# Normalising x by rows and turning it on TensorE, in the front of a hybrid attention layer

## The chip, the core and the metric

The kernel runs on one core of one Trainium2 chip. Time is device time in microseconds (us) of one execution; the kernel before took 860.34 us, the median of three runs (858.98 to 860.87). The engines are called PE (TensorE, with PEld for its weight loads), DVE (VectorE), ACT (ScalarE), POOL (GpSimd) and SP (SyncE, which here only issues transfers).

## What is computed

One layer over x (512 tokens, 1024 channels) and mem (256 memory tokens): three attention branches (gated linear attention "GLA", forgetting attention "FoX", cross attention into mem), merged by gates, an output projection, a squared-ReLU MLP and a last norm. The parts that the change touches:

```python
def rmsnorm(x, g):
    r = lax.rsqrt(jnp.mean(xf * xf, axis=-1, keepdims=True) + EPS)
    return (xf * r) * g

u = rmsnorm(h, g_mix[l])                    # h = x here
proj = u @ w_in[l]                          # feeds all three branches
...
mkv = rmsnorm(mem, g_mem[l]) @ w_mem_kv[l]
mk, mv = jnp.split(mkv, 2, axis=-1)         # memory keys, memory values
```

## The kernel before, in words

All matrix products run in a split of float32 into a high and a low part (`hi`, `lo`, type fp32r), three matmuls for each product (`mm3`, L122 to L124). A weight chunk of 128x1024 floats (512 KB) is loaded by SP (`load_w`, L108), its `hi` is cast on ACT (L114) and its `lo` is subtracted on DVE (L115); the pools hold three chunks of `raw`, of `hi` and of `lo`, so a cast into the fourth waits until PE has done with the first. `gT` makes one feature tile by tokens (one step for each of 8 contraction tiles); `gN` makes tokens by 512 features, chunk after chunk, with one PSUM bank for each token tile.

PE's order is the order of the code. The other engines' instructions are ordered by a scheduler when the program is built; `tc.issue_after(...)` keeps a group of them behind a given instruction.

The front (the pool `front`, L238 to L340) goes like this:

- mem and x come feature-major (features on partitions, `memr` and `xr`). SP loads mem in four parts between the parts of key chunk 0, then key chunks 1 and 2, half of x, chunk 3, the other half of x, chunk 4 (the first of the values), constants, and the later chunks.
- mem's values times the gain are split into `mxh` and `mxl` without the norm's factor, which is put in afterwards.
- `mk_proj` (L308) makes memory keys of one head; between the four of them, ACT squares mem and x and POOL and DVE add the squares up (`sq_cols`, L177). `rms_cols` (L189) sums over the partitions by matmuls with a column of ones (L195), and `rsqrt` (L198) makes a mean on DVE and a power of -0.5 on POOL. `bcast_rows` (L205) brings these factors to all partitions as a row: a diagonal matrix on ACT (L210), a matmul with ones (L211), a copy (L212).
- The memory values (`mv`, L325) are 48 matmuls over four chunks, with x's sum and x's row of factors between them.
- Then, for each of 8 feature tiles, u = x times gain times row is made on DVE or POOL (L335, L337) and split into `uhi` (ACT) and `ulo` (DVE).
- `g_proj` (L361) is the first product that wants u: 16 matmuls (L369, L370) for the low-rank decay and forget columns.

Behind the front, `fox_pair(0)` (L425) makes queries and keys of the first two FoX heads, 48 matmuls; `mem_split` (L342) puts mem's factors into the memory keys and splits keys and values. `decay_logs` (L380) makes log-sigmoids from the gate columns: four small matmuls (L383), absolute values, exponentials, and logarithms on ACT, the last with a load of another function table. `v_chunks` (the values of FoX, called `fv`) needs four PSUM banks of the pool `pmm`, which has four; the last one that comes free is that of the FoX keys, when `k_evac` (L438) has copied the second half out of it.

Of the kernel before, what the change touches and what calls it, by code (L numbers as in the profile page):

```python
# [58 lines left out]


@with_exitstack
def hybrid_block(ctx, tc, chunks, wst, xT, memT, xN, cols, gffn, gfin, wup, cst, out):
    nc = tc.nc
    PSUM = bass.MemoryType.PSUM
    index = {c: i for i, c in enumerate(chunks)}
# [3 lines left out]
    def nm(s):  # L69
        uid[0] += 1  # L70
        return f"{s}_{uid[0]}"
# [13 lines left out]
    def at_(shape=None):  # L85
        return pa.tile(shape or [P, 512], F32, tag="a", name=nm("a"))
# [67 lines left out]
    def run(*gens):  # L154
        for g in gens:
            for _ in g:
                pass
# [16 lines left out]
        nc.scalar.copy(hi, src)  # L174
        return nc.vector.tensor_tensor(lo, src, f(hi), op=ALU.subtract).ins  # L175

    def sq_cols(pool_, src, n, k, accs, pool_ks, tag):  # L177

        e = 1 if k in pool_ks else 0
        eng = nc.gpsimd if e else nc.vector  # L180
        if accs[e] is None:
            accs[e] = pool_.tile([P, n], F32, tag=f"{tag}_acc{e}", name=nm("acc"))
            nc.scalar.activation(accs[e], src[:, k, :], AF.Square)
        else:
            sq = pool_.tile([P, n], F32, tag=f"{tag}_sq{e}", name=nm("sq"), bufs=2)
            nc.scalar.activation(sq, src[:, k, :], AF.Square)
            eng.tensor_tensor(accs[e], accs[e], sq, op=ALU.add)

    def rms_cols(pool_, accs, n):  # L189

        accs = [a for a in accs if a is not None]
        ps = at_()
        for t in range(n // P):
            for i, a in enumerate(accs):
                nc.tensor.matmul(ps[:, t:t + 1], a[:, t * P:(t + 1) * P], ones[:, 0:1], start=i == 0, stop=i == len(accs) - 1)  # L195
        return rsqrt(pool_, ps[:, :n // P], 1.0 / D, n // P)

    def rsqrt(pool_, ss, inv, n):  # L198
        ms = pool_.tile([P, n], F32, tag="ms", name=nm("ms"), bufs=2)
        r = pool_.tile([P, n], F32, tag="rr", name=nm("rr"), bufs=2)  # L200
        nc.vector.tensor_scalar(ms, ss, inv, EPS, op0=ALU.mult, op1=ALU.add)
        nc.gpsimd.tensor_tensor(r, ms, mhalf[:, :n], op=ALU.pow)
        return r
# [33 lines left out]

    with pool("front") as fp:  # L238
        rmb = gv[:, 0, 0:M]
        rxb = fp.tile([P, S], F32, name="rxb")  # L240
        memr = fp.tile([P, KT, M], F32, name="memr")
        xr = fp.tile([P, KT, S], F32, name="xr")
        pre = {}

        def lead(key, n, i):
            if key not in pre:
                late = index[key] > 2
                pre[key] = [(fp if late else wp).tile([P, 1024], F32, tag="lead" if late else "raw", name=nm("raw"),
                                                      bufs=2 if late else 3)]
                pre[key] += [wp.tile([P, 1024], F32R, tag=g, name=nm(g)) for g in ("hi", "lo")]  # L250
            sl = slice(i * 1024 // n, (i + 1) * 1024 // n)
            raw, hi, lo = (t[:, sl] for t in pre[key])
            nc.sync.dma_start(raw, wst[index[key]][:, sl])
            nc.scalar.copy(hi, raw)
            nc.vector.tensor_tensor(lo, raw, f(hi), op=ALU.subtract)
# [12 lines left out]
        macc, xacc = [None, None], [None, None]  # L268
# [18 lines left out]
        nc.sync.dma_start(wup_s, wup)  # L287
        nc.sync.dma_start(cmask, cst[:, 6 * P + 8:])
        for k in range(KT):
            sq_cols(fp, memr, M, k, macc, range(KT), "m")  # L290
# [7 lines left out]
        UP = (2, 5)  # L298
# [6 lines left out]
        def mk_raw(h):  # L305
            return gkT[h // 2][:, (h % 2) * M:(h % 2) * M + M]

        def mk_proj(h):  # L308
            run(gT(("T", "w_mem_kv", P * h), mxh, mxl, lambda ps: nc.scalar.copy(mk_raw(h), ps[:, :M]), n=M))
            for k in (2 * h, 2 * h + 1):  # L310
                sq_cols(fp, xr, S, k, xacc, (1, 2, 3), "x")
                if k in UP:
                    nc.scalar.mul(xr[:, k, :], xr[:, k, :], gmix[:, k:k + 1])

        def mv_evac(t, ps):
            nc.scalar.mul(gqT[t], ps, rm[:, t:t + 1])

        mk_proj(0)
        mk_proj(1)
        rm = rms_cols(fp, macc, M)  # L320
        mk_proj(2)
        bcast_rows(fp, rm, M, rmb)
        mk_proj(3)
        nc.vector.tensor_copy(msk_s.rearrange("p a b -> p (a b)"), cst_s[:, 4 * P:6 * P])
        mv = gN([("N", "w_mem_kv", 2 * j, 512) for j in range(4)], of(mxh, mxl), 2, mmt, mv_evac)  # L325
        for _ in range(2):
            next(mv)
        rx = rms_cols(fp, xacc, S)
        for _ in range(5):
            next(mv)  # L330
        bcast_rows(fp, rx, S, rxb)
        for k in range(KT):
            ut = fp.tile([P, S], F32, tag="ut", name=nm("ut"), bufs=3)
            if k in UP:
                nc.gpsimd.tensor_tensor(ut, xr[:, k, :], rxb, op=ALU.mult)  # L335
            else:
                nc.vector.scalar_tensor_tensor(ut, xr[:, k, :], gmix[:, k:k + 1], rxb, op0=ALU.mult, op1=ALU.mult)  # L337
            u_end = split(uhi[:, k, :], ulo[:, k, :], ut)
        run(mv)
        get_w = get_plain  # L340

        def mem_split():  # L342
            for h in range(4):
                mk_evac(h)
            for t in range(2):
                split(mvh[:, t, :], mvl[:, t, :], gqT[t])

# [4 lines left out]
    with pool("fox") as xp:  # L352
# [668 lines left out]
def layout(inputs):  # L1021
# [26 lines left out]
    def tl(a):  # L1048
# [22 lines left out]
    cst[:, 6 * P:6 * P + 8] = -0.5  # L1071
    cst[:, 6 * P + 8:] = np.where(t > s, np.float32(NEG), 0.0)
    arrays = {
        "wst": wst, "xT": tl(x), "memT": tl(mem), "xN": np.ascontiguousarray(x), "cols": cols,
        "gffn": np.ascontiguousarray(np.broadcast_to(np.asarray(inputs["g_ffn"])[0], (P, D))),
        "gfin": np.ascontiguousarray(np.broadcast_to(np.asarray(inputs["g_final"]), (P, D))),
        "wup": wup, "cst": cst,
# [24 lines left out]
```

## Time and profile before

| what | value |
|---|---|
| time before, median of three runs | 860.34 us (858.98 to 860.87) |
| the profiled execution's own time | 859.26 us |
| its span in the trace | 857.1 us |
| PE busy / DVE busy / ACT busy / POOL busy | 840.5 / 498.4 / 404.3 / 87.4 us |
| mean granted PE clock | 0.995 |
| moved by DMA | 108.28 MB |

The span is what the trace shows from the first to the last instruction; the other 2.16 us lie around it. Matmuls are pipelined and their ends are modelled, so the distance of two starts tells more than a length. A bracket behind an instruction gives the idle time of its engine just before, and what ended it. The granted clock is TensorE's, as a share of full speed. Times in the timeline count from the start of the span.

### The profile page before, as it was taken

What the parts mean: (1) busy time and instruction counts of PE and PEld (TensorE: products, weight loads), DVE (VectorE), ACT (ScalarE), POOL (GpSimd) and SP (SyncE); (2) the same over time, 40 slices, a digit from 0 to 9 for tenths busy, and PEclk for the clock granted to TensorE, in tenths of its full rate; (3) what the DMA queues carried; (4) which work ended last, traced back from release to release, by engine and by line L of the source; (5) the groups of instructions that cost most, each with busy time, mean ns of one, the idle gap of its engine ahead of it and who ended that gap; (6) DMA issues with size and microseconds to landing.
All of it is one profiled execution on the core that took longest, in us unless ns stands there. A gap on an engine that the chain in (4) does not pass through costs nothing.

```text
span 857.1 us, 10630 instructions
## 1 busy us (share of the span) xinstructions
PE 840.5 (98%) x4041; PEld 695.4 (81%) x4041; DVE 498.4 (58%) x832; ACT 404.3 (47%) x646; POOL 87.4 (10%) x96
## 2 busy tenths in 40 slices
PE   8899999999999999999999999999999999999995
PEld 5778788888888888787888889888888888888884
DVE  5775657766444556574533546665556645665577
ACT  8764747754332431322332434655455345535642
POOL 5100000000000011211112100011001000110022
PEclk9999999999999999999999999999999999999998
DMA  8433232322222122124222413969435933791156
GB/s 319 151 123 125 106 115 99 123 75 75 76 96 99 53 96 75 50 74 172 99 98 99 172 50 124 318 122 238 155 97 122 273 123 83 149 281 53 26 102 168
DMA packets 32146, 108.28 MB, mean 126 GB/s; under 512 B 3872, under 2 KB 4832, under 8 KB 32096
## 3 DMA queue, kind: packets, MB, share of 16 engines
q1 hardware_dynamic: 24832, 84.00, 27.3%
q0 software_dynamic: 5472, 18.35, 12.2%
q10 hardware_dynamic: 1792, 5.26, 1.8%
q8 instruction: 32, 0.52, 0.2%
q14 instruction: 18, 0.15, 0.1%
HBM read 103.90 MB, written 2.13 MB: 124 GB/s over the span
## 4 chain that ended last, share of the span: by engine, by line
PE 90%; ACT 3%; DVE 3%; DMA 1%; issue 1%; POOL 0%; SPq 0%; DVEq 0%; POOLq 0%; ACTq 0%
PE mm L122 25%; PE mm L123 24%; PE mm L124 24%; PE a L123 3%; PE a L124 3%; PE a L122 3%; PE a L739 1%; DMA h<-G 1%; PE a L756 1%; PE a L499 1%; PE a L498 1%; PE a L750 1%; DMA memr<-in_memT_dram 1%; PE a L467 1%; PE a L466 1%
## 5 line engine op out<-in xcount | busy, mean ns | idle before, releaser
L115 DVE TENSOR_TENSOR wlo<-raw,whi 128x1024 fp32r<-128x1024 f32 x103 | 129.9, 1264 | 133.4 <-ACT whi L114 131.7
L114 ACT CAST whi<-raw 128x1024 fp32r<-128x1024 f32 x103 | 108.4, 1053 | 168.6 <-PE mm L123 128.4
L122 PE MATMUL mm<-uhi,whi 128*128 128x512 f32 x352 | 139.7, 397 | 0.0
L124 PE MATMUL mm<-uhi,wlo 128*128 128x512 f32 x352 | 137.6, 391 | 0.0
L123 PE MATMUL mm<-ulo,whi 128*128 128x512 f32 x352 | 137.5, 391 | 0.0
L122 PE MATMUL mm<-u2h,whi 128*128 128x512 f32 x240 | 93.4, 389 | 0.0
L123 PE MATMUL mm<-u2l,whi 128*128 128x512 f32 x240 | 93.4, 389 | 0.0
L124 PE MATMUL mm<-u2h,wlo 128*128 128x512 f32 x240 | 93.4, 389 | 0.0
L175 DVE TENSOR_TENSOR lo<-raw,hi 128x1024 fp32r<-128x1024 f32 x42 | 51.2, 1224 | 49.6 <-ACT hi L174 49.1
L124 PEld LDWEIGHTS mm<-uhi,wlo 128*128 128x128 f32 x352 | 66.2, 188 | 14.2
L122 PEld LDWEIGHTS mm<-uhi,whi 128*128 128x128 f32 x352 | 66.4, 189 | 13.5 <-issue 0.7
L123 PEld LDWEIGHTS mm<-ulo,whi 128*128 128x128 f32 x352 | 66.3, 188 | 12.9
L174 ACT CAST hi<-raw 128x1024 fp32r<-128x1024 f32 x42 | 44.0, 1053 | 62.5 <-PE mm L123 23.5
L979 POOL DMA_DIRECT2D raw<-in_wst_dram x32 | 28.1, 877 | 277.2 <-DVE lo L175 208.0
L123 PEld LDWEIGHTS mm<-u2l,whi 128*128 128x128 f32 x240 | 45.0, 188 | 9.4
L122 PEld LDWEIGHTS mm<-u2h,whi 128*128 128x128 f32 x240 | 45.0, 188 | 9.3
L124 PEld LDWEIGHTS mm<-u2h,wlo 128*128 128x128 f32 x240 | 45.0, 188 | 9.3
L122 PE MATMUL mm<-hi,ch 128*128 128x512 f32 x120 | 46.7, 389 | 0.0
L123 PE MATMUL mm<-lo,ch 128*128 128x512 f32 x120 | 46.7, 389 | 0.0
L124 PE MATMUL mm<-hi,cl 128*128 128x512 f32 x120 | 46.7, 389 | 0.0
L590 POOL TENSOR_TENSOR acc<-acc,th 128x512 f32<-128x512 f32 x16 | 24.0, 1503 | 102.7 <-DVE th L589 102.7
L668 POOL MEMSET qpos<- 64x512 f32 x2 | 1.0, 524 | 268.6 <-PE mm L124 268.6
(320 smaller groups left out, 1641.1 us busy)
## 6 DMA issues: line engine op xcount, KB each, us to landing
raw<-in_wst_dram SPq DMA_DIRECT2D x144, 512.0 KB
raw<-in_wst_dram POOLq DMA_DIRECT2D x32, 512.0 KB, 5.3
nFb<-dF ACTq DMA_DIRECT2D x8, 512.0 KB
xr<-in_xT_dram SPq DMA_DIRECT2D x4, 512.0 KB
h<-in_xN_dram SPq DMA_DIRECT2D x4, 512.0 KB
memr<-in_memT_dram SPq DMA_DIRECT2D x4, 256.0 KB
h<-G POOLq DMA_DIRECT2D x4, 256.0 KB, 5.7
out_dram<-h ACTq DMA_DIRECT2D x4, 256.0 KB
```

Of the source, the lines that this page charges most:

```text
L114: nc.scalar.copy(hi, raw)
L115: nc.vector.tensor_tensor(lo, raw, f(hi), op=ALU.subtract)
L122: nc.tensor.matmul(ps, lh, rh, start=start, stop=False)
L123: nc.tensor.matmul(ps, lh, rl, start=False, stop=False)
L124: nc.tensor.matmul(ps, ll, rh, start=False, stop=stop)
L174: nc.scalar.copy(hi, src)
L175: return nc.vector.tensor_tensor(lo, src, f(hi), op=ALU.subtract).ins
L466: nc.tensor.matmul(ps[:, :w], q, K[e][:, 0, :w], start=True, stop=False)
L467: nc.tensor.matmul(ps[:, :w], q, K[e][:, 1, :w], start=False, stop=True)
L498: nc.tensor.matmul(po[:, q0:], vv, PTh[:, c0:c0 + w], start=n == 0, stop=False)
L590: nc.gpsimd.tensor_tensor(acc[j], acc[j], th, op=ALU.add)
L979: nc.gpsimd.dma_start(raw[to, i], wst[index["B", q, i, x]], accum_op=ALU.add)
```

## The change

- x is no longer loaded feature-major; it comes as it is (`xn`, tokens on partitions, four tiles of 128 tokens, 512 KB each, from `xN`), behind key chunk 3 instead of around it.
- Between the four key projections, `x_norm(t)` squares a token tile on ACT with the sum along the row, makes the factor (`rsqrt`, mean on DVE and power on POOL), and scales the tile in place on DVE.
- `u_turn(k)` turns one feature tile: four PE transposes into one PSUM bank, then ACT writes `uhi` (times gain) and DVE writes `ulo`, both from PSUM. Two of them stand ahead of each chunk of the memory values.
- The four key projections stay in their PSUM banks until ACT copies them out behind the last `uhi`. The values use two banks of the pool `pa` instead of `pmm`, and are copied out without the factor.
- mem's statistics move: two squares on ACT (1024 wide) behind the last `uhi`, three additions on DVE; sum and factor (`mem_rms`) on PE behind `g_proj`; the row of factors (`mem_rows`) behind the first step of `fox_pair(0)`; `mem_split` behind that pair.

```diff
-        for j in range(4):
-            nc.sync.dma_start(xr[:, 2 * j:2 * j + 2], xT[:, 2 * j:2 * j + 2])
-            if j == 1:
-                lead(chunks[3], 1, 0)
+        lead(chunks[3], 1, 0)
+        for t in range(NT):
+            nc.sync.dma_start(xn[:, t, :], xN[t * P:(t + 1) * P, :])
         lead(chunks[4], 1, 0)
...
+        def x_norm(t):
+            sq = fp.tile([P, D], F32, tag="xsq", name=nm("xsq"), bufs=2)
+            nc.scalar.activation(sq, xn[:, t, :], AF.Square, accum_out=ssx[:, t:t + 1])
+            r = rsqrt(fp, ssx[:, t:t + 1], 1.0 / D, 1)
+            nc.vector.tensor_scalar(xn[:, t, :], xn[:, t, :], r, None, op0=ALU.mult)
+
+        def u_turn(k):
+            pt = at_()
+            for t in range(NT):
+                nc.tensor.transpose(pt[:, t * P:(t + 1) * P], xn[:, t, k * P:(k + 1) * P], ident)
+            a = nc.scalar.mul(uhi[:, k, :], pt, gmix[:, k:k + 1]).ins
+            return a, nc.vector.scalar_tensor_tensor(ulo[:, k, :], pt, gmix[:, k:k + 1], f(uhi[:, k, :]), op0=ALU.mult,
+                                                  op1=ALU.subtract).ins
+
+        for h in range(4):
+            mk_proj(h)
+            x_norm(h)
+        mv = gN([("N", "w_mem_kv", 2 * j, 512) for j in range(4)], of(mxh, mxl), 2, at_, lambda t, ps: nc.scalar.copy(gqT[t], ps))
+        for k in range(KT):
+            u_act, u_end = u_turn(k)
+            if k % 2:
+                run(islice(mv, 4))
+        with tc.issue_after(u_act):
+            for h in range(4):
+                nc.scalar.copy(mk_raw(h), kps[h][:, :M])
+        run(mv)
...
+        macc, rm, dg = gv[:, 2, :M], gv[:, 1, :2], gv[:, 3, :M]
+        msq = [fp.tile([P, 4, M], F32, name=f"msq{h}") for h in range(2)]
+        with tc.issue_after(u_act):
+            for h in range(2):
+                nc.scalar.activation(msq[h], memr[:, 4 * h:4 * h + 4, :], AF.Square)
+        nc.vector.tensor_tensor(msq[0], msq[0], msq[1], op=ALU.add)
+        nc.vector.tensor_tensor(msq[0][:, :2, :], msq[0][:, :2, :], msq[0][:, 2:, :], op=ALU.add)
+        nc.vector.tensor_tensor(macc, msq[0][:, 0, :], msq[0][:, 1, :], op=ALU.add)
+
+        def mem_rms():
+            ps = at_()
+            for t in range(2):
+                nc.tensor.matmul(ps[:, t:t + 1], macc[:, t * P:(t + 1) * P], ones[:, 0:1], start=True, stop=True)
+            nc.vector.tensor_scalar(rm, ps[:, :2], 1.0 / D, EPS, op0=ALU.mult, op1=ALU.add)
+            nc.gpsimd.tensor_tensor(rm, rm, mhalf[:, :2], op=ALU.pow)
+            for t in range(2):
+                nc.scalar.mul(dg[:, t * P:(t + 1) * P], ident, rm[:, t:t + 1])
+
+        def mem_rows():
+            pb = at_()
+            for t in range(2):
+                sl = slice(t * P, (t + 1) * P)
+                nc.tensor.matmul(pb[:, sl], ones, dg[:, sl], start=True, stop=True)
+            nc.scalar.copy(rmb, pb[:, :M])
...
         g_proj()
+        mem_rms()
...
         with tc.issue_after(u_end):
             next(pair)
-            mem_split()
+            mem_rows()
         run(pair)
+        mem_split()
         decay_logs()
```

More of the change, by code (lines that the diff above doesn't have):

```diff
@@ L61, in hybrid_block @@
 @with_exitstack
-def hybrid_block(ctx, tc, chunks, wst, xT, memT, xN, cols, gffn, gfin, wup, cst, out):
+def hybrid_block(ctx, tc, chunks, wst, memT, xN, cols, gffn, gfin, wup, cst, out):
     nc = tc.nc
@@ L175, in split @@
         return nc.vector.tensor_tensor(lo, src, f(hi), op=ALU.subtract).ins
[L177 to L196, printed above, removed]
     def rsqrt(pool_, ss, inv, n):
@@ L239, in hybrid_block @@
         rmb = gv[:, 0, 0:M]
-        rxb = fp.tile([P, S], F32, name="rxb")
         memr = fp.tile([P, KT, M], F32, name="memr")
-        xr = fp.tile([P, KT, S], F32, name="xr")
+        xn = fp.tile([P, NT, D], F32, name="xn")
+        ssx = small(fp, NT, "ssx")
         pre = {}
@@ L297, in hybrid_block @@
         get_w = get_first
-        UP = (2, 5)
         def mk_evac(h):
@@ L306, in mk_raw @@
             return gkT[h // 2][:, (h % 2) * M:(h % 2) * M + M]
+        kps = []
         def mk_proj(h):
[L309 to L323, printed above, removed]
-        nc.vector.tensor_copy(msk_s.rearrange("p a b -> p (a b)"), cst_s[:, 4 * P:6 * P])
[L325 to L339, printed above, removed]
-        get_w = get_plain
+            run(gT(("T", "w_mem_kv", P * h), mxh, mxl, kps.append, n=M))
@@ L345, in mem_split @@
             for t in range(2):
-                split(mvh[:, t, :], mvl[:, t, :], gqT[t])
+                nc.scalar.mul(mvh[:, t, :], gqT[t], rm[:, t:t + 1])
+                nc.vector.scalar_tensor_tensor(mvl[:, t, :], gqT[t], rm[:, t:t + 1], f(mvh[:, t, :]), op0=ALU.mult,
+                                               op1=ALU.subtract)
     with pool("fox") as xp:
@@ L1073, in layout @@
     arrays = {
-        "wst": wst, "xT": tl(x), "memT": tl(mem), "xN": np.ascontiguousarray(x), "cols": cols,
+        "wst": wst, "memT": tl(mem), "xN": np.ascontiguousarray(x), "cols": cols,
         "gffn": np.ascontiguousarray(np.broadcast_to(np.asarray(inputs["g_ffn"])[0], (P, D))),
```

3 lines of the change are left out of this document (removed).

## The prediction

> **What bounds the kernel now.** I read the chain of waits first, then the stages in windows, then PE's timeline, and only then the engines that feed PE.
>
> ```profile
> span 857.1 us, 10630 instructions
> PE 90%; ACT 3%; DVE 3%; DMA 1%; issue 1%; POOL 0%; SPq 0%; DVEq 0%; POOLq 0%; ACTq 0%
> ```
>
> PE's own work is nine tenths of the chain, so the end is set by PE's dense stream: whatever moves PE at the end of the front moves the end of the kernel. Below, PE's timeline through the front (start, length, idle before and its releaser in brackets).
>
> ```profile
> 16.50 0.61 PE L195 MATMUL a<-cst_s,acc 128*128 128x1 f32 x4 [0.20 <-POOL acc L187]
> 16.97 0.36 PE L122 MATMUL mm<-mxh,hi 128*128 128x256 f32 x1
> 19.92 0.61 PE L211 MATMUL a<-dg,cst_s 128*128 128x128 f32 x4
> 23.50 0.39 PE L122 MATMUL mm<-hi,mxh 128*128 128x512 f32 x1
> 32.26 0.48 PE L122 MATMUL mm<-whi,mxh 128*128 128x512 f32 x1
> 38.50 0.39 PE L369 MATMUL mm<-uhi,whi 128*128 128x512 f32 x1
> 41.15 0.50 PE L370 MATMUL mm<-ulo,whi 128*128 128x512 f32 x1 [0.90 <-DVE ulo L175]
> 42.53 0.50 PE L370 MATMUL mm<-ulo,whi 128*128 128x512 f32 x1 [0.65 <-DVE ulo L175]
> 57.35 1.94 PE L383 MATMUL a<-wup_s,gaT 128*128 128x264 f32 x8
> 58.93 0.59 PE L122 MATMUL mm<-whi,uhi 128*128 128x512 f32 x1
> 64.37 0.47 PE L122 MATMUL mm<-whi,uhi 128*128 128x512 f32 x1 [0.99 <-DVE K L175]
> ```
>
> The keys end at 23.50 and the memory values at 38.50; 27 of their matmuls from 32.26 take 6.24 us, 0.23 each. The gate projection (16 matmuls, 3.7 us dense) stands waiting for u, and the first FoX pair is over at 57.35. I compare everything at that mark: from there PE's order is the same in both programs.
>
> The same stretch in windows; the columns are the window, its length, busy time of PE, PEld, DVE, ACT and POOL, the granted clock, the DMA share and GB/s:
>
> ```profile
> 38.50:47.10 8.60, 6.98 (x20) 4.28 (x19) 8.51 (x13) 6.44 (x11) 1.79 (x3) 0.80 0.04 14
> 47.10:57.50 10.40, 10.40 (x47) 8.60 (x46) 8.32 (x14) 4.66 (x10) 0.00 (x0) 1.00 0.58 202
> 64.40:75.00 10.60, 10.60 (x49) 8.73 (x50) 5.08 (x17) 5.63 (x9) 0.00 (x0) 1.00 0.15 51
> ```
>
> A mean of 0.80 over 8.60 us is 3.4 us at half speed: after idling 0.90 and 0.65 us PE lost half its clock. That dip costs up to 3.4 / 2 = 1.7 us, and lies inside the 57.35. The wait of 0.99 us before 64.37 was followed by none (1.00 in the third row); so the point lies between 1.0 and 1.55 us of idleness close together.
>
> **The change, part by part.** It takes L195 and L211 out of the keys, normalises x by rows, turns it by 32 PE transposes between the value chunks, and puts mem's statistics behind the gate projection.
>
> *x arrives later.* SP's queue gives landing times, because in the built program an issue waits for the transfer eight before it on that queue:
>
> ```profile
> 12.49 0.33 SPq L287 DMA_DIRECT2D wup_s<-in_wup_dram  x1
> 13.76 0.33 SPq L288 DMA_DIRECT2D cst_s<-in_cst_dram  x1
> 15.12 55.27 SPq L108 DMA_DIRECT2D raw<-in_wst_dram  x13
> ```
>
> 12.49 is the landing of chunk 2, 13.76 that of x's first quarter, 15.12 of its second: 1.3 us for each 512 KB. The changed queue has chunk 3 ahead of four x tiles of the same size, so chunk 3 lands at 13.8 and x at 15.1, 16.4, 17.7 and 18.95. Chunk 4, the constants and chunks 5 to 7 follow; chunk 5 at about 22.4 is wanted at 27, so the values are covered. If that cover went, each late us would be a us of PE.
>
> The durations that I use, grouped by line and shape (busy, then mean ns):
>
> ```profile
> L114 ACT CAST whi<-raw 128x1024 fp32r<-128x1024 f32 x16 | 16.7, 1051 | 17.0 <-PE mm L123 8.3 <-PE mm L124 7.4 <-issue 1.2
> L186 ACT ACTIVATE sq<-xr 128x512 f32<-128x512 f32 x6 | 3.5, 618 | 0.0
> L316 ACT ACTIVATE gqT<-mm,rr 128x512 f32<-128x512 f32 x2 | 1.4, 676 | 0.0
> L309 ACT COPY gkT<-mm 128x256 f32<-128x256 f32 x4 | 1.5, 364 | 0.2 <-PE mm L124 0.2
> L210 ACT ACTIVATE dg<-cst_s,rr 128x128 f32<-128x128 f32 x6 | 2.1, 395 | 3.7 <-POOL rr L202 2.8 <-PE a L211 0.8
> L115 DVE TENSOR_TENSOR wlo<-raw,whi 128x1024 fp32r<-128x1024 f32 x15 | 18.2, 1222 | 15.8 <-ACT whi L114 15.8
> L175 DVE TENSOR_TENSOR ulo<-ut,uhi 128x512 fp32r<-128x512 f32 x8 | 5.2, 684 | 0.1
> L393 DVE TENSOR_TENSOR la<-la,sg 128x256 f32<-128x256 f32 x4 | 1.7, 420 | 0.0
> L475 DVE TENSOR_SCALAR Pt<-Pt,ri 128x512 f32<-128x512 f32 x2 | 1.0, 483 | 0.0
> L201 DVE TENSOR_SCALAR ms<-a 128x4 f32<-128x4 f32 x1 | 0.2, 161 | 0.1
> L804 POOL TENSOR_TENSOR rr<-ms,cst_s 128x1 f32<-128x1 f32 x8 | 4.9, 617 | 53.3 <-DVE ms L803 53.1
> ```
>
> *Normalising x.* No row has a square over 1024 with its sum: between 1.05 (a cast of that size) and 1.24 (two of 512), and I take 1.2, since the sum is read out behind it. The scaling over 1024 lies between 0.48 (half the size) and 0.97 (two of them); 0.76, as about 0.2 of each is fixed. In the built program DVE's order is mean, scale, mean, scale, tile after tile, so a tile costs 0.16 + 0.6 + 0.76 + hand-overs = 1.55, more than the 1.3 between landings. First square over at 16.4, and four tiles: x is ready at 22.6 (21.8 if only the last tile counted). The keys lose L195 (16.50 to 16.97 and its wait of 0.20) and up to 0.6 at L211: they end at 22.2 to 22.5. So the first transpose goes at about 22.6, 0.9 earlier than the values began before. What went with POOL's sums and ACT's squares was hidden and is worth nothing beyond that.
>
> *The turns.* From the scores of a FoX head:
>
> ```profile
> 114.38 0.60 PE L482 MATMUL a<-cst_s,Pt 128*128 128x128 f32 x4
> 115.39 0.47 PE L122 MATMUL mm<-uhi,whi 128*128 128x512 f32 x1
> ```
>
> Between these two starts stand ten such turns (L482 x4, L484 x1, L486 x3, L489 x2) in 115.39 - 114.38 = 1.01 us, and the matmul behind them loses 0.1: 0.115 each, at most the 0.15 of a row by itself (0.60 / 4). 32 take 3.7 (to 4.8). With 48 value matmuls (11.0), 16 of the gate (3.7) and 0.3 of hand-overs PE ends the gate at 22.6 + 18.7 = 41.3. Evacuations keep up: a pair of u tiles is 1.2 us of ACT and 1.3 of DVE, with one cast (1.0) and one subtraction (1.2) beside it, in a period of 3.7; a late one would hold the next pair's bank. The four key banks, now held until ACT's copies behind the last uhi (about 37), are free before 38. So u no longer stalls the gate.
>
> *What is late next: mem's statistics.* ACT's order in the built program, from the end of the third value chunk at 33.95, is: cast of fq's weights, two uhi, four key copies, two squares of mem (1024 each), two value copies, cast of fk's weights. That is 1.0 + 1.2 + 1.1 + 1.9 + 1.2 + 1.05 = 7.4, to about 41.4; on DVE fk's subtraction (1.22) and the last sum (0.42) stand behind that cast: 42.75. PE wants the sum at 41.3 for mem_rms, and everything queued behind it waits: 1.5 us idle. Then 0.5 for mem_rms and 0.7 for the three matmuls of the pair's first step. mem_rows needs the diagonals: cast of fv's weights (1.05, it waits for the gate's buffer at 41.3), its subtraction (1.22), mean (0.16), pow (0.6), two diagonals (0.7), hand-overs 0.4: 45.5. PE idles another 1.6. The turn of the rows takes 0.5 (bounds 0.4 to 0.6, L211), 45 matmuls of the pair 10.3: the mark is at 56.4, against 57.35: -0.95 at full clock. Both waits could be 0.8 shorter or longer together, as the sum of 13 ACT and DVE pieces can be off by 0.1 each.
>
> *The clock.* Before, 1.55 us of idleness in two pieces brought 3.4 us at half speed; here 1.5 and 1.6 stand 1.2 apart, and 45 dense matmuls behind them to pay. I put one dip here: between 0 and 1.7, 1.5 taken, as it can begin while PE still idles. [...]
>
> *The second K evacuation.* The fourth value bank of fv is the bank of K. ACT before, behind the mark:
>
> ```profile
> 58.43 0.58 ACT L174 CAST K<-mm 64x512 fp32r<-64x512 f32 x1
> 59.56 1.20 ACT L384 ACTIVATE sg<-a 128x264 f32<-128x264 f32 x4
> 60.78 1.05 ACT L388 ACTIVATE sg<-sg 128x264 f32<-128x264 f32 x3
> 61.86 1.05 ACT L441 CAST K<-K 64x1024 fp32r<-64x1024 f32 x1
> 62.92 0.58 ACT L174 CAST K<-mm 64x512 fp32r<-64x512 f32 x1
> 63.96 1.28 ACT L390 ACT_TABLE_LOAD   x1
> 65.26 1.37 ACT L390 ACTIVATE sg<-sg 128x264 f32<-128x264 f32 x4
> ```
>
> The second K cast came before the table load. In the built changed program, ACT runs all four exponentials, the table load and one logarithm first, and only Q's last copy (the 0.5 us between the first two rows) has gone from ahead of it. Added: 0.35 + 1.28 + 0.35 (a quarter of 1.37); gone: 0.5; PE is let on 1.5 us later (bounds 1.0 and 2.0). The wait of 0.99 becomes some 2.5, long enough for a second dip, 0 to 1.7, 1.5 taken.
>
> *Sum:* -0.95 + 1.5 + 1.5 + 1.5 = +3.55 us. The profiled execution ran 859.26 us (span 857.1 and 2.16 around it), which gives 862.8. The median shown is 860.34, 1.08 above it, which gives 863.9; I take 863.3.
>
> **The rivals.**
>
> [...]
> - *One dip of the two:* +2.05, 861.9. [...]
> - *Faster:* mem's statistics are ready in time. If the sum is there by 41.3 and the diagonals by 42.5, the 3.1 us of idleness and the first dip go, and K's 1.5 stays without its dip: -0.95 - 3.1 + 1.5 = -2.55, 857.2. It takes ACT 1.5 us faster over seven rows than they show; against it, too, the fv cast cannot start before the gate ends.
> - *x late:* four tiles at 1.6 instead of 1.3 land 1.2 later, and the turns shift one for one, with a third dip if PE idles over 1.5 at 22: +1.2 to +2.9 on the forecast, 864.5 to 866.2. It decides once x's last tile lands after 18.6.
>
> **How the numbers follow.** Forecast with both dips 0.42, one dip 0.20, none 0.12, faster 0.14, x late 0.12. A change under 0.2% (1.7 us, 858.6 to 862.1) can't be told from none here. Faster: the 0.14 and a little of the no-dip case, 0.17. Within: no dips, most of one dip and the forecast's lower edge, 0.30. Slower: 0.53. The forecast's own range is 861.5 to 865; reaching to the other cases until two in ten are out: 858.8 to 866.0.
>
> **What would show it.** Right: the first transpose near 22.6; no wait of the gate matmuls for ulo; PE idle some 1.5 us at mem_rms (for the sum) and at mem_rows (for the diagonals); a granted clock of 0.5 behind them; a wait of over 2 us for K behind the table load, 8.5 us after the mark. Wrong: PE dense from 23 to the mark, with that at 54; a clock of 1.00 throughout; or a first transpose behind 24.

## The result and the profile after

| | before | after |
|---|---|---|
| median (lowest to highest), 11 runs each | 860.17 us (858.86 to 861.43) | 864.10 us (859.87 to 866.04) |
| the profiled execution's own time | 859.26 us | 864.10 us |
| its span | 857.1 us | 862.2 us |
| mean granted PE clock | 0.995 | 0.992 |

The ratio after to before is 1.0040, with a 95% interval of 1.0024 to 1.0055: the changed kernel is slower by 0.4%, 0.8 us above the predicted 863.3 and well inside its range.

PE's timeline of the changed kernel through the front (start, length, idle before and its releaser in brackets):

```profile
22.26 0.49 PE L296 MATMUL a<-cst_s,xn 128*128 128x128 f32 x3
23.08 0.77 PE L296 MATMUL a<-cst_s,xn 128*128 128x128 f32 x5 [0.33 <-DVE xn L290]
...
30.66 1.03 PE L296 MATMUL a<-cst_s,xn 128*128 128x128 f32 x8
31.45 0.48 PE L122 MATMUL a<-whi,mxh 128*128 128x512 f32 x1
...
37.88 0.39 PE L372 MATMUL mm<-uhi,whi 128*128 128x512 f32 x1
...
43.32 0.58 PE L329 MATMUL a<-cst_s,gv 128*128 128x1 f32 x4 [1.65 <-DVE gv L323]
...
45.65 0.78 PE L340 MATMUL a<-gv,cst_s 128*128 128x128 f32 x4 [0.94 <-ACT gv L333]
...
58.09 1.94 PE L387 MATMUL a<-wup_s,gaT 128*128 128x264 f32 x8
...
66.47 0.47 PE L122 MATMUL mm<-whi,uhi 128*128 128x512 f32 x1 [2.34 <-DVE K L175]
...
73.64 0.30 PE L402 MATMUL a<-lf,cst_s 128*128 128x32 f32 x2
```

The turns start at 22.26; the 32 of them are woven into the values, and the gate projection starts at 37.88 and runs without a wait for u (before: 38.50, with waits of 0.90 and 0.65). Up to there the changed kernel is ahead. Then PE stands 1.65 us for mem's sum and 0.94 us for the diagonals, and the mark (L387 here, L383 before) comes at 58.09 against 57.35: what was ahead is 0.74 behind. At the bank of K the wait is 2.34 us where it was 0.99, and the distance is 66.47 - 64.37 = 2.10.

The same kernel in windows (window, length, busy time of PE, PEld, DVE, ACT and POOL, granted clock, DMA share, GB/s):

```profile
45.65:52.00 6.35, 6.35 (x23) 5.19 (x24) 4.10 (x10) 3.13 (x8) 0.00 (x0) 0.73 0.27 82
66.40:77.00 10.60, 10.53 (x42) 8.52 (x43) 3.63 (x15) 3.66 (x5) 0.00 (x0) 0.84 0.14 51
67.00:70.40 3.40, 3.40 (x9) 2.63 (x8) 1.07 (x4) 1.78 (x2) 0.00 (x0) 0.50 0.00 0
```

Two dips: 0.73 over 6.35 us and 0.84 over 10.60 us are each 6.35 x 0.27 = 10.60 x 0.16 = 1.7 us of full speed lost, and the last row is the second dip alone, 3.4 us at half speed. Before there was one, and PE ran at 1.00 behind K. Distances to the kernel before, at starts of the same matmuls:

| matmul | before | after | distance |
|---|---|---|---|
| the mark, first of the gate's four | 57.35 | 58.09 | +0.74 |
| bank of K | 64.37 | 66.47 | +2.10 |
| sums of the log-gates | 69.94 | 73.64 | +3.70 |
| a turn of the MLP's input | 512.13 | 516.20 | +4.07 |

The 0.37 between the last two rows is mainly one wait at 164.38 (0.29 us, for another K). The span grew by 5.1, 1.0 more than 4.07. That last 1.0 is in the final transfer; VectorE's timeline before, and then after:

```profile
843.29 0.69 DVE L931 TENSOR_TENSOR h<-h,R 128x512 f32<-128x512 f32 x1 [1.62 <-DMA h<-G]
```

```profile
848.33 0.69 DVE L936 TENSOR_TENSOR h<-h,R 128x512 f32<-128x512 f32 x1 [2.60 <-DMA h<-G]
```

In the fourteen profiled executions of this study this wait is either 1.3 to 1.6 us or 2.5 to 2.9 us, and two variants of the kernel before, both below, fall on either side of the gap (1.63 and 2.46); so I don't count it as the change's, though whether the change makes the longer one likelier is open. The medians are 3.9 apart, near the 4.07.

### The profile page after: what moved, and what is told of

It is laid out like the page before. It is cut to its first block, busy times and chain, and to the rows that moved or that the text cites. A ratio compares the mean times of both kernels' runs of the same rounds, so it can differ in the third digit from the quotient of the medians.

```text
span 862.2 us, 10621 instructions
## 1 busy us (share of the span) xinstructions
PE 842.0 (98%) x4049; PEld 697.4 (81%) x4049; DVE 492.5 (57%) x832; ACT 401.3 (47%) x633; POOL 75.2 (9%) x88
## 4 chain that ended last, share of the span: by engine, by line
PE 86%; ACT 5%; DVE 4%; DMA 3%; issue 1%; POOL 1%; SPq 0%; DVEq 0%; POOLq 0%; ACTq 0%
PE mm L122 23%; PE mm L123 23%; PE mm L124 23%; PE a L123 3%; PE a L124 3%; PE a L122 3%; DVE wlo L115 1%; ACT whi L114 1%; DMA nFb<-dF 1%; PE a L744 1%; DMA h<-G 1%; DMA xn<-in_xN_dram 1%; DMA raw<-in_wst_dram 1%; PE a L761 1%; PE a L755 1%
## 5 line engine op out<-in xcount | busy, mean ns | idle before, releaser
L122 PE MATMUL mm<-whi,uhi 128*128 128x512 f32 x64 | 26.4, 412 | 2.6 <-DVE K L175 2.6
```

The source lines that it names most:

```text
L122: nc.tensor.matmul(ps, lh, rh, start=start, stop=False)
```

## The experiments

Two causes are on trial: mem's statistics behind the gate (waits of 1.65 and 0.94 and the first dip), and the second half of K's evacuation behind the table load (2.34 and the second dip). Rivals: x came late; or the turns (the 32 transposes on PE) are dear by themselves. Times are medians of 5 to 12 runs, each compared with the kernel before on the same chip (859.62 to 860.11 us). This table is the key to what follows: starts in each profiled execution, as above.

| kernel | mark | sums | MLP turn | median | ratio to before (95%) |
|---|---|---|---|---|---|
| before | 57.35 | 69.94 | 512.13 | 860.17 | |
| after | 58.09 | 73.64 | 516.20 | 864.10 | 1.0040 (1.0024 to 1.0055) |
| K first | 57.57 | 70.14 | 513.44 | 862.84 | 1.0041 (1.0027 to 1.0055) |
| statistics late | 52.56 | 66.86 | 510.35 | 859.23 | 0.9989 (0.9977 to 1.0000) |
| both | 52.14 | 64.70 | 510.46 | 857.52 | 0.9972 (0.9961 to 0.9983) |
| fillers | 56.28 | 70.19 | 512.72 | 859.69 | 0.9997 (0.9987 to 1.0008) |
| x behind chunk 4 | 58.89 | 74.39 | 516.93 | 865.08 | 1.0058 (1.0036 to 1.0080) |
| before, K late | 56.93 | 73.25 | 515.47 | 863.53 | 1.0040 (1.0027 to 1.0053) |

### K's evacuation ahead of the logarithms

Both halves of K leave their bank before anything else is done with them, and the log-gates are held behind that.

```diff
...
                 for e, a, b in rows:
-                    split(K[e][a, 0, :], K[e][a, 1, :], ps[a])
+                    k_act[j] = nc.scalar.copy(K[e][a, 0, :], ps[a]).ins
+                    nc.vector.tensor_tensor(K[e][a, 1, :], ps[a], f(K[e][a, 0, :]), op=ALU.subtract)
+                for e, a, b in rows:
                     nc.scalar.copy(K[e][b, :, :], f(K[e][a, :, :]))
...
-        decay_logs()
+        with tc.issue_after(k_act[0]):
+            decay_logs()
```

> Changed kernel with FoX's second key evacuation put ahead of the logs (both K casts behind each other, decay_logs issued behind the second). Theory (a wait behind the table load, then a clock dip): the idle 2.34 us before PE's fourth fv bank goes, and with it the dip of 3.4 us at half clock at 67; PE is 2.3 + 1.5 = 3.8 us earlier behind it, about 860.3 us against 864.1, and the dip at 46.7 stays. Rival (x's later start carries the loss): no more than the 1.4 us by which that wait grew, about 862.7, or nothing.

In the profiled execution the wait of 2.34 and the dip behind it are gone, and the sums come 3.5 us earlier than after the change. But this execution (861.56 us) is the second fastest of its twelve. The median fell by only 1.3 us, and by the ratio to the kernel before nothing was gained: 1.0041 against 1.0040. The number is nearer to the rival's 862.7 than to the theory's 860.3. PE's timeline of this run:

```profile
70.14 0.41 PE L402 MATMUL a<-lf,cst_s 128*128 128x32 f32 x2 [1.10 <-DVE lf L395]
...
101.23 0.33 PE L488 MATMUL a<-cst_s,Pt 128*128 128x128 f32 x1 [1.01 <-DVE Pt L481]
```

Two new waits stand in place of the old one: the log-gates, now last on ACT, are late for their sums (1.10), and the reordering, which holds for every pair, puts the next pair's second K subtraction (99.96 on DVE) there ahead of the last scaling of scores (1.01). The cure moved the wait: 1.10 and 1.01 stand for 2.34. So this run does not show what the wait for K cost; the next one and the run with both edits do.

### The same delay put into the kernel before

Here the kernel before is made to do what the scheduler did to the changed one: K's second half is held behind the first logarithm, and so behind the table load.

```diff
...
+                half(*rows[0])
+                if j:
+                    half(*rows[1])
+                else:
+                    later.append(partial(half, *rows[1]))
...
-        decay_logs()
+        with tc.issue_after(decay_logs()):
+            later[0]()
```

> Kernel before, with only the second key evacuation of the first FoX pair put behind the fourth exponential, the table load and one logarithm, as the changed kernel's ACT order has it. Theory: 0.35 + 1.28 + 0.35 = 2.0 us added to PE's wait of 0.99 for that bank, so 3.0 idle, and a dip behind it: +2.0 to +3.5, 861.7 to 863.2 us against 859.7. Rival (the wait's growth in the changed kernel is a mere shift from the front): no change of the time.

The kernel before becomes 0.4% slower, 3.9 us: as much as the whole change. PE's line at the bank, and two windows:

```profile
66.15 0.77 PE L122 MATMUL mm<-whi,uhi 128*128 128x512 f32 x1 [3.19 <-DVE K L175]
```

```profile
41.20:51.20 10.00, 8.86 (x32) 5.78 (x33) 9.75 (x16) 5.89 (x11) 0.34 (x2) 1.00 0.19 58
66.10:76.10 10.00, 9.95 (x39) 8.09 (x40) 3.37 (x14) 3.16 (x4) 0.00 (x0) 0.83 0.15 52
```

The wait is 2.2 longer than the 0.99 of before, and a dip of 1.7 comes with it: 3.9. (In this execution, at 862.62 us the fastest of its eleven, the MLP turn is 3.34 later than before; it has no dip at the gate.) So an evacuation behind the table load costs this much with x, turns and statistics left as they were. It is 0.3 above the upper end of what was expected, since the wait became 3.19, longer than the changed kernel's 2.34. The first window shows something else: gate waits of 0.87 and 0.66, as in the kernel before, without a dip in this execution, and yet the mark (56.93) is only 0.42 earlier than before.

### mem's statistics later

The sum goes behind 14 steps of FoX's values, where the log-gates' sums stand too, and the rows and `mem_split` some steps further; nothing wants them before cross attention.

```diff
         g_proj()
-        mem_rms()
...
             next(pair)
-            mem_rows()
         run(pair)
-        mem_split()
         decay_logs()
...
         run(islice(fv, 14))
+        mem_rms()
...
+        run(islice(fv, 6))
+        mem_rows()
+        mem_split()
         run(fv)
```

> Changed kernel with mem's statistics on PE put into the FoX values (mem_rms behind 14 steps of fv, mem_rows and mem_split eight steps later) instead of behind the gate. Theory: the two waits (1.65 and 0.94 us by the trace, 2.9 by starts) and the dip behind them go, the mark (first of the four gate matmuls) comes at 54 instead of 58.1, and the time falls by about 4 us to 860; the wait for K and its dip stay. Rival (x's later start, or the 32 turns, carry the loss): the mark moves by less than 1.5 us.

The median falls by 4.9 us (4.4 by the two ratios) and the MLP turn comes 5.85 earlier. PE's timeline and a window:

```profile
52.56 1.94 PE L386 MATMUL a<-wup_s,gaT 128*128 128x264 f32 x8
...
60.94 0.47 PE L122 MATMUL mm<-whi,uhi 128*128 128x512 f32 x1 [2.35 <-DVE K L175]
```

```profile
61.00:71.00 10.00, 10.00 (x49) 8.28 (x50) 4.91 (x17) 5.20 (x9) 0.70 (x1) 1.00 0.15 52
```

Neither statistics wait is left, and the mark is 5.53 earlier: 2.59 of waits, 1.7 of dip, and mainly the statistics' own matmuls (43.75 - 43.32 and 46.18 - 45.65 after the change, 1.0 together), which now lie behind it. The wait for K is what it was (2.35), but no dip followed it in this execution.

### Both

The two edits together.

> Both edits together. Theory: the losses add, 3.8 + 4.1 = 7.9 us, about 856.2 us, which is 4 us below the kernel before (860.2), with no granted clock of 0.5 between 20 and 110 us. Rival: no better than the better one of the two alone, since something else (x's arrival, a weight load) then sets PE's pace.

857.52 us: 0.28% faster than before, and 0.7% faster than the changed kernel by the two ratios. That is 1.3 above what was expected, so the gains don't add up as priced; but next to the statistics alone, the K edit is worth 1.7 us here (859.23 to 857.52, twelve runs each). Two waits of the K edit are left:

```profile
64.70 0.41 PE L401 MATMUL a<-lf,cst_s 128*128 128x32 f32 x2 [0.76 <-DVE lf L394]
...
96.27 0.33 PE L487 MATMUL a<-cst_s,Pt 128*128 128x128 f32 x1 [1.01 <-DVE Pt L480]
```

In this execution the clock was also 0.83 between 90 and 100 us, which takes back what the earlier sums had gained; it ran 858.95 us, the slowest of its twelve. The mark at 52.14, 5.2 earlier than before (1.0 of it the statistics' matmuls, now behind the mark), speaks against the rival of dear turns: the 3.2 us of the turns (32 of 0.1) are more than paid for in the front, once nothing waits behind it.

### The waits filled with useless matmuls

The changed kernel, with matmuls whose result nobody reads: 6 ahead of mem's sum, 3 ahead of its rows, 8 among the values ahead of K's bank. All waits for data stay; only PE's idleness goes.

```diff
+        def keep_busy(n):
+            ps = at_()
+            for _ in range(n):
+                nc.tensor.matmul(ps, uhi[:, 0, :P], uhi[:, 0, :], start=True, stop=True)
+
         g_proj()
+        keep_busy(6)
         mem_rms()
...
```

> Changed kernel with dummy matmuls (128x512, result unused) in the three waits: 6 ahead of mem_rms, 3 ahead of mem_rows, 8 ahead of the fourth fv bank, each a little shorter than the wait it stands in. The waits themselves stay. Theory (idleness halves the clock, and that costs 1.5 us each time): both dips go and the time falls by about 3 us to 861, the mark from 58.1 to 56.6. [...]

Doing 17 matmuls more makes the kernel 4.4 us faster (3 were expected), level with the kernel before. PE's timeline, and windows over both places:

```profile
43.10 0.58 PE L329 MATMUL a<-cst_s,gv 128*128 128x1 f32 x4 [0.30 <-DVE gv L323]
...
45.44 0.78 PE L340 MATMUL a<-gv,cst_s 128*128 128x128 f32 x4 [0.27 <-ACT gv L333]
...
64.67 0.47 PE L122 MATMUL mm<-whi,uhi 128*128 128x512 f32 x1 [0.54 <-DVE K L175]
```

```profile
41.00:65.00 24.00, 22.90 (x103) 18.24 (x103) 15.42 (x35) 17.34 (x35) 0.71 (x1) 1.00 0.26 90
64.60:75.00 10.40, 10.33 (x48) 8.59 (x49) 4.61 (x15) 3.69 (x5) 0.00 (x0) 1.00 0.15 54
```

Sum and rows come within 0.25 us of when they did, and K's bank at the same distance (64.67 is 8.39 behind the mark; 8.38 after the change), and the clock is 1.00 throughout: the MLP turn is 3.48 earlier, the 3.4 of two dips. (The other 1 us between the profiled executions is the last transfer again: VectorE waited 0.27 and 1.30 for it here.) The runs tell the same: the changed kernel's spread over 6.2 us (859.87 at a mean clock of 0.996, 866.04 at 0.986), these over 1.3 us (858.97 to 860.25). That the executions of the changed kernel differ by how many dips they take is what these numbers suggest.

### x one transfer later

```diff
         lead(chunks[3], 1, 0)
+        lead(chunks[4], 1, 0)
         for t in range(NT):
             nc.sync.dma_start(xn[:, t, :], xN[t * P:(t + 1) * P, :])
-        lead(chunks[4], 1, 0)
```

> Changed kernel with x loaded behind chunk 4 instead of ahead of it, that is one 512 KB transfer (1.3 us) later. Theory (x's arrival sets the first transpose, one for one): first transposes 1.3 us later, at 23.6 for the first three and 24.4 for the rest, the mark (four gate matmuls) from 58.1 to 59.4, time +1.3 us, 865.4. Rival (x has slack): mark and time unchanged. If instead idleness before the turns brings a third dip: +2.8.

```profile
22.50 0.33 PE L296 MATMUL a<-cst_s,xn 128*128 128x128 f32 x1 [0.81 <-DVE xn L290]
24.25 0.77 PE L296 MATMUL a<-cst_s,xn 128*128 128x128 f32 x5 [1.42 <-DVE xn L290]
```

PE waits 0.81 and 1.42 for the normalised tiles where it waited 0.33, the second group of turns starts 1.17 later (24.25 against 23.08), the mark comes 0.80 later, and the median is 1.0 higher. About two thirds of x's lateness reach the mark, and the changed kernel as it is has 0.33 us of it; it isn't where the 3.9 went.

### The idleness of the kernel before

If dips are so dear, the kernel before should gain when its own (behind the gate's waits for `ulo`) is filled: three useless matmuls behind the fourth `uhi` matmul of the gate, two behind the fifth.

```diff
+            pd = at_()
             for k in range(KT):
                 nc.tensor.matmul(ps, w[:, k, :], uhi[:, k, :], start=k == 0, stop=False)
+                for _ in range({3: 3, 4: 2}.get(k, 0)):
+                    nc.tensor.matmul(pd, uhi[:, 0, :P], uhi[:, 0, :], start=True, stop=True)
```

> Kernel before, with dummy matmuls (128x512, result unused) in the gate projection where PE waits for ulo: 3 in the wait of 0.90, 2 in that of 0.65. The waits for u stay. Theory (1.55 us of idleness halved the clock for 3.4 us): no dip at 43.7, the mark comes 1.2 to 1.7 us earlier than 57.35, time about 858.3 against 859.7. Rival (the dip costs nothing, or comes for another reason): the dip stays and the time is 859.7 or later.

It lost instead: 861.45 us, ratio 1.0015 (1.0001 to 1.0028). The dip is gone and the mark comes at 56.85, but only 0.5 earlier: the gate's `ulo` come from DVE one by one, and PE now stands three times about 0.2 at them, and 0.17 at a weight. The kernel before with K late took no dip there either, without filling, and its mark was 0.42 earlier. So the dip of the kernel before cost about 0.5 us, and not the 1.7 that half speed could cost. And the MLP turn is at 512.69, 0.56 later than before. PE's timeline shows where, and DVE's shows why:

```profile
160.82 0.47 PE L122 MATMUL mm<-whi,uhi 128*128 128x512 f32 x1 [0.94 <-DVE K L175]
```

```profile
155.66 0.76 DVE L458 TENSOR_TENSOR nFb<-nFb,cst_s 128x128 f32<-128x128 f32 x2 [1.83 <-DMA nFb<-dF]
156.34 1.22 DVE L115 TENSOR_TENSOR wlo<-raw,whi 128x1024 fp32r<-128x1024 f32 x1
157.59 0.68 DVE L175 TENSOR_TENSOR K<-mm,K 64x512 fp32r<-64x512 f32 x1
```

DVE stands at the mask's addition to a head's forget bias, which comes from DRAM; behind it are a weight subtraction and K's evacuation, and PE wants K's bank. ACT issued this transfer at 151.22 here and at 151.64 in the kernel before; it was over at 155.66 here and at 155.15 there, 4.44 us against 3.51. (The 0.29 at 164.38 after the change is the same place.) Two runs went after it. The first asks for each bias one head earlier:

```diff
...
-            nFb = xp.tile([P, 8, P], F32, tag="nFb", name=nm("nFb"), bufs=2)
-            nc.scalar.dma_start(nFb, dF[h:h + 1, :].to_broadcast([P, 8 * P]))
+            nFb = bias.pop(h) if h else load_bias(0)
...
+            if h < 7:
+                bias[h + 1] = load_bias(h + 1)
```

> The kernel before with the five filling matmuls, and each head's forget bias asked for one head earlier. Theory (DVE stands on the bias transfer, which landed 4.44 us after its issue, with K's evacuation queued behind it): the wait of 0.94 us at 160.8 goes, the u2 turn comes at about 511.75 in place of 512.69, and the median falls from 861.45 to about 860.5. Rival (K is late by its own chain, or by the extra bank): the wait stays, 861.4.

862.71 us, ratio 1.0040 (1.0028 to 1.0053), and the wait stayed (0.91 us at 161.61; the whole front was 0.8 later in this execution). The trace shows why this tells nothing of the cause: the edit moved no transfer. Issue for issue, the heads' transfers go 0.8 us later than without it, as the whole front does (the seventh at 152.00 against 151.22), the seventh addition stands at 156.46 against 155.66, and DVE waited 1.85 us for it. Why it is 1.3 us slower than without the edit is open. The second run takes the addition off DVE:

```diff
-                nc.vector.tensor_tensor(nFb[:, b, :], nFb[:, b, :], m, op=ALU.add)
+                nc.gpsimd.tensor_tensor(nFb[:, b, :], nFb[:, b, :], m, op=ALU.add)
```

> The kernel before with the five filling matmuls, and the mask added to the forget bias on POOL in place of DVE, so that no instruction of DVE stands on the bias transfer. Theory (K's evacuation was queued on DVE behind that wait): the 0.94 us at 160.8 goes, the u2 turn comes some 0.5 before the kernel before (near 511.7), median 860.5. Rival (K is late by ACT's chain of its own): the wait stays within 0.2 of 0.94, 861.4.

DVE's timeline now:

```profile
154.90 1.23 DVE L115 TENSOR_TENSOR wlo<-raw,whi 128x1024 fp32r<-128x1024 f32 x1 [1.03 <-ACT whi L114]
156.16 0.68 DVE L175 TENSOR_TENSOR K<-mm,K 64x512 fp32r<-64x512 f32 x1
```

The subtraction of K starts at 156.16 in place of 157.59, PE's wait of 0.94 is gone, and the MLP turn is at 511.75, as expected; the median is 860.26, 1.2 us below the run without this edit. So in these executions the loss sat at this addition. For the medians it isn't settled: the intervals of the two ratios overlap, and the addition on POOL was not tried in the kernel before without filling. With both, the kernel is level with before (1.0004, 0.9995 to 1.0013): filling the kernel before brings nothing measurable, in agreement with a dip that cost it only 0.5 us.

### Versions faster than the kernels before and after

A gentler form of "both": only pair 0's evacuation is reordered, and the statistics stand 3 steps apart from the log-gates' sums and rows. The difference to "both":

```diff
                     nc.vector.tensor_tensor(K[e][a, 1, :], ps[a], f(K[e][a, 0, :]), op=ALU.subtract)
-                for e, a, b in rows:
-                    nc.scalar.copy(K[e][b, :, :], f(K[e][a, :, :]))
+                    if j:
+                        nc.scalar.copy(K[e][b, :, :], f(K[e][a, :, :]))
+                if j == 0:
+                    for e, a, b in rows:
+                        nc.scalar.copy(K[e][b, :, :], f(K[e][a, :, :]))
...
         mem_rms()
+        run(islice(fv, 3))
         decay_sums()
...
-        run(islice(fv, 6))
+        run(islice(fv, 3))
         mem_rows()
```

> As the run with both edits, but only the first pair's key evacuation is reordered (the second pair's copies stand as in the changed kernel), and the forget sums come three steps of fv later, behind the logs. Theory: the new waits that the trace of the run with both edits shows (0.8 us for lf at the sums, 1.0 us for the scaled scores at 96, and a dip of the clock around 92) go: 0.8 + 1.0 + up to 1.5, so about 854.5 to 855.5 us against 857.5. Rival (those waits are hidden or reappear one step later): 857.5 again.

857.90 us, ratio 0.9974 (0.9962 to 0.9986), no better than "both" and 2.4 above the upper end of what was expected: the waits of 0.76 and 1.01 are gone, but in their place stand a wait of 1.78 us for the forget columns at 70.89, one of 0.56 for a K at 158.52, and a half-clock stretch of 6.8 us early in the front of this execution. With the bias asked for one head earlier:

> The changed kernel with both causes mended in the gentler form (857.9 us), and the bias asked for one head earlier. Theory: its one later wait of 0.6 us for a FoX key goes too, 857.3. Rival (those waits have covers of their own, or the earlier transfers delay the weights): 857.9 or above.

857.54 us, 0.9977 (0.9968 to 0.9985): the 0.56 is not in its profile, but the medians can't be told apart. With the mask's addition on POOL:

> The changed kernel with both causes mended in the gentler form (857.9 us) and the mask added on POOL. Theory: the later wait of 0.56 us for a FoX key goes, 857.3. Rival (POOL's additions are slower than DVE's and come late for the scores): a new wait at the scores, 858 or above.

856.36 us in five runs, ratio 0.9955 (0.9942 to 0.9969), the best of all: 0.45% faster than before and 0.9% faster than the changed kernel, and 0.9 us below what was expected. Between 24 and 200 us PE has one wait over 0.3, that at the forget columns (1.78 us at 69.48). Its windows from x on:

```profile
14.00:41.00 27.00, 26.38 (x163) 23.12 (x163) 19.39 (x27) 21.36 (x32) 2.62 (x6) 1.00 0.69 251
41.00:69.00 28.00, 26.70 (x122) 21.90 (x120) 15.84 (x38) 18.21 (x32) 0.70 (x1) 1.00 0.29 97
69.40:79.40 10.00, 9.92 (x46) 8.29 (x47) 5.79 (x12) 4.80 (x11) 1.43 (x2) 1.00 0.48 154
```

The clock is whole from 14 to 79. How the 1.5 us to the gentler form divide between the missing K wait and the missing half-clock stretch is open; the two ran on different occasions, and each is compared with before by its own ratio.

## Why the prediction was right

**x's arrival and the turns.** Right, 0.4 late. The queue, the squares and the scaling of the changed kernel, by SP's timeline (the transfer that waits for chunk 2), ACT's (the first square) and DVE's (the last two tiles):

```profile
13.12 0.33 SPq L264 DMA_DIRECT2D wup_s<-in_wup_dram  x1
...
15.69 1.06 ACT L288 ACTIVATE xsq<-xn 128x1024 f32<-128x1024 f32 x1 [0.17 <-DMA xn<-in_xN_dram]
...
20.73 0.76 DVE L290 TENSOR_SCALAR xn<-xn,rr 128x1024 f32<-128x1024 f32 x1 [0.73 <-POOL rr L181]
...
22.27 0.75 DVE L290 TENSOR_SCALAR xn<-xn,rr 128x1024 f32<-128x1024 f32 x1 [0.73 <-POOL rr L181]
```

The landing that the prediction put at 12.49 was 13.12, and the first x tile was there at 15.7 instead of 15.1. From then on the steps were as priced: the square with its sum took 1.18, from 15.69 to the mean on DVE at 16.87 (1.2), the scaling 0.75 (0.76), a tile 22.27 - 20.73 = 1.54 (1.55), so x was ready at 23.0 (22.6). PE didn't lose the 0.4, since three tiles' turns went ahead of the last tile's. Eight turns took 31.45 - 30.66 = 0.79, 0.1 each (0.115). The gate ended at 43.32 - 1.65 = 41.67 (41.3).

**The first wait.** Right: 1.65 us against 1.5, for the sum, as named. DVE's timeline:

```profile
41.61 1.22 DVE L115 TENSOR_TENSOR wlo<-raw,whi 128x1024 fp32r<-128x1024 f32 x1
42.75 0.42 DVE L323 TENSOR_TENSOR gv<-msq 128x256 f32<-128x256 f32 x1
43.09 1.22 DVE L115 TENSOR_TENSOR wlo<-raw,whi 128x1024 fp32r<-128x1024 f32 x1
44.22 0.15 DVE L330 TENSOR_SCALAR gv<-a 128x2 f32<-128x2 f32 x1
```

The last sum stands behind a weight's subtraction, at 42.75 to 43.17; the prediction had it over at 42.75. On ACT the work ahead of that, from the cast of fq's weights to that of fk's, began at 34.47 (33.95) and took 7.1 (7.4). Two of the prediction's prices there lie below its own rows, four key copies at 1.1 where the row has 1.5, and two squares at 1.9 where two casts of that size take 2.1; they measured 1.19 and 2.05.

**The second wait.** Mechanism right, size off: 0.94 instead of 1.6. The diagonals ended within 0.15 of the predicted 45.5, since the mean stood behind another subtraction (44.22, above). But PE came to them later, at 45.65 - 0.94 = 44.71 instead of 44.0: the sum was 0.5 late, and what lies between took 1.39 instead of 1.2. The two waits together are 2.59 against 3.1.

**The first dip.** Right in this execution: 1.7 lost in the window (1.5). With it the mark was at +0.74 against the predicted -0.95 + 1.5 = +0.55.

**K's second evacuation.** Right in cause and size. ACT's timeline behind the mark:

```profile
59.26 0.58 ACT L174 CAST K<-mm 64x512 fp32r<-64x512 f32 x1
59.74 1.21 ACT L388 ACTIVATE sg<-a 128x264 f32<-128x264 f32 x4
60.84 1.36 ACT L392 ACTIVATE sg<-sg 128x264 f32<-128x264 f32 x4
62.22 1.28 ACT L394 ACT_TABLE_LOAD   x1
63.51 0.42 ACT L394 ACTIVATE sg<-sg 128x264 f32<-128x264 f32 x1
63.96 1.04 ACT L445 CAST K<-K 64x1024 fp32r<-64x1024 f32 x1
65.02 0.58 ACT L174 CAST K<-mm 64x512 fp32r<-64x512 f32 x1
```

From the first K cast (59.26) to the second (65.02) ACT does the exponentials, the table load and a logarithm; the bank was free 66.47 - 58.09 = 8.38 us behind the mark (predicted 8.5; before 7.02), 1.36 later than before where 1.5 was taken.

**The second dip.** Right in this execution: from the bank to the sums the distance grew by 3.70 - 2.10 = 1.60 (1.5). Gaps of 1.65 and 0.94 and one of 2.34 were followed by half speed here, and the longest gap between matmuls, in any run, behind which it fell was 3.19. Without its two dips of 1.5 the forecast would have been 3.0 lower, 860.3, which is what the fastest executions came near (859.87 and 860.92).

**The luck in it.** The prediction put the point between 1.0 and 1.55 us of idleness close together. The runs show no such point: a wait of 2.35 passed without a dip (statistics late), as did 0.87 and 0.66 (before, K late). The eleven runs tell how often each case came. Here the mean clock of a profiled execution is 0.996 to 0.998 without a dip, 0.994 to 0.995 with one and 0.992 to 0.993 with two or one double. By that estimate three of the eleven had none (0.996; 859.87 to 861.54 us), one had one and seven had two or more. The forecast, which gave both dips 0.42, hit the commonest case; that the profiled execution and the median are of this case was partly luck.

**The sum.** +0.74, +1.36 and +1.60 make 3.70 where 3.55 was forecast. The further 0.37 (the bias transfer's K wait, mainly) had no term; with it, 4.07, and 3.9 in the medians. With the median of the 11 runs, 860.17, the sum gives 863.7.

**The rivals.** x late: of a delay, two thirds reached the mark (0.80 of 1.17) where one for one was priced, and the delay (0.33 us of waiting) was small. Its sign was set too low: the last tile will have landed after 18.6, since ACT got the third at 18.30, but the forecast itself had 18.95, and by its own 21.8 against 22.6 a landing up to 19.7 is covered. Faster: it said that with the statistics in time the kernel would be 6.1 us below the forecast; moving them took 4.9 off the median, to 859.23, so it named the larger lever.

## What to carry to other kernels

When PE's work is nine tenths of the chain that ended last (90% here), price a reordering by what comes next in line on the engines that free its banks: here an evacuation that let PE on 1.4 us later, and a small statistic that nothing wants until cross attention, put where PE had to wait for it at once, took more than a real gain in the front. Move such small things far behind their inputs, and evacuate a bank before a table load, not behind it; but look again at the order afterwards, as the first cure made two new waits. An idle gap of PE costs its length and, in some executions, up to 1.7 us more. Useless matmuls in it can buy that back (4.4 us in the changed kernel), but not where PE is held by another engine at the same place (the gate of the kernel before).

## What the runs showed of the hardware

- The granted clock fell to half for 3.4 us behind idle pieces of 0.90 and 0.65 us (before), 1.65 and 0.94, and 2.34 (after), 3.19 (before with K late), and 0.28, 0.25 and 1.01 (both); and in two executions early, while the first weights were cast (from 9.8 us on with the bias early, mean clock 0.994, and from 11.0 on for 6.8 us, twice 3.4, in the gentler form, mean clock 0.993). It did not fall behind 2.35 (statistics late), 1.78 (the best version), 0.81 and 1.42 (x behind chunk 4), nor behind 0.87 and 0.66 (before with K late, the same place in which the kernel before took its dip). Idleness alone doesn't settle it.
- The wait just ahead of a dip does not set when it starts. Below are the starts of the two dips in windows of 0.1 us, after the change and then with x behind chunk 4 (the clock is the third number from the end; 0.67 means half speed for two thirds of the window):

```profile
46.50:46.60 0.10, 0.10 (x2) 0.10 (x1) 0.00 (x0) 0.10 (x1) 0.00 (x0) 0.67 0.82 287
67.00:67.10 0.10, 0.10 (x2) 0.09 (x1) 0.10 (x1) 0.10 (x1) 0.00 (x0) 0.57 0.00 0
```

```profile
46.60:46.70 0.10, 0.10 (x2) 0.10 (x2) 0.00 (x0) 0.10 (x2) 0.00 (x0) 0.93 0.24 41
67.10:67.20 0.10, 0.00 (x0) 0.00 (x0) 0.07 (x2) 0.10 (x2) 0.00 (x0) 0.82 0.00 0
```

They start at 46.53 and 67.01, and at 46.69 and 67.16: 20.48 us apart both times, six times the 3.41 that each of three dips lasted (43.66 to 47.07 before, 46.53 to 49.94 and 67.01 to 70.43 after). Behind the wait for the diagonals the dip starts 0.88 us after its end in the changed kernel (46.53; 45.65), 0.23 after it with x later (46.69; 46.46), and 0.15 before it with K first (45.12; 45.27; the clock was 0.65 from 45.20 to 50.00). Two pairs of dips are too few for a rule. How busy PE was just ahead doesn't settle it either: in the 3.41 us ahead of the dip it was busy for 1.85 in the kernel before (40.24 to 43.65), and for 2.28 (43.12 to 46.53) and 1.07 (63.60 to 67.01) in the changed one, where 3.41 us with 1.96 of work (39.71 to 43.12) were followed by full speed (1.00 from 43.12 to 46.53).

- Filling those gaps held the clock at 1.00 and narrowed the spread of the runs from 6.2 to 1.3 us.
- One and the same transfer of a head's forget bias took 3.51 us in one execution and 4.44 in another, and the last transfer of the kernel made DVE wait either about 1.5 or about 2.7 us. DVE took its instructions in order here (a weight's subtraction stood behind the addition until 156.34, and started at 154.90 where the addition was on POOL), so such a spread can reach PE. Both versions with the addition on POOL, where a pair took 1.4 to 2.5 us against 0.76 on DVE, have medians 1.2 and 1.5 us below their like without it; the intervals of the ratios overlap in both pairs.
